# A hybrid attention and gating layer on one core: three kinds of 128-column matmul go from three rounded products to one unrounded product

## The chip, the cores and the metric

The kernel runs on 1 core of one Trainium2 chip. The time is device microseconds (us) of one execution; the median of 3 runs is 1607.43 us (1607.42 to 1607.93). The engines are named as in the profile: PE (TensorE matmuls), PEld (its weight loads), DVE (VectorE), ACT (ScalarE), POOL (GpSimd) and SP (SyncE, which here issues DMAs). A trailing q, as in SPq, is the engine's queue.

## The reference

One layer with 512 tokens of 2048 features and 16 heads, all in 32-bit floats. Cut to what matters:

```
proj = h @ w_in                       # q_lat, kv_lat, k_rope, z, u, v, ...
q    = rmsnorm(q_lat) @ w_uq          # 16 heads, 128 + 64 rotary
kv   = rmsnorm(kv_lat) @ w_ukv        # 16 heads, key 128 + value 128
s    = (q_nope . k_nope + q_rope . k_rope) / sqrt(192), causal, softmax -> p
A    = (p @ v) * silu(z_mla)
mixed = tril(W_s[g]) @ v_chunk + b_s  # 16 groups, 4 chunks of 128 tokens
B    = u * mixed * silu(z_sgu)
out  = rmsnorm(x + gate * ((sigmoid(g_mla) A + sigmoid(g_sgu) B) @ w_out))
```

The change touches three products: the gating mix (`tril(W_s) @ v_chunk`), the scores (`q_nope . k_nope`) and the product with the values (`p @ v`).

## The kernel before, in words

**Rounded pairs.** A 32-bit operand x is split into a rounded part h and the remainder l = x - h (`hilo`, L140: ACT copies x to h with rounding, then DVE subtracts). A product a·b is then three matmuls, ah·bh + ah·bl + al·bh, added up in PSUM (`mm3`, L135 to L138). Every operand that PE reads has to pass ACT and then DVE first. Two products, L441 and L1079, are done unrounded: one matmul instruction on 32-bit operands, which the trace shows as two records, each with its own weight load.

**The stages, in order of time.** To about 345 us: conditioning and the first projections. From 348 to about 1130 us: 266 *slots* (loop at L1276), in each of which PE does 16 or 24 matmuls (L1289 to L1297) of the rest of the input projection. From about 1137 to 1433 us: attention, one head after another (loop at L1523). Then the output projection.

**What orders the slots.** The side work on DVE and ACT is put into slots by a planner (`place`, L590). Each job brings a planned cost in us of DVE time, and goes to the first slot whose planned DVE time stays under 2.7 (2.6 for slots of 16 matmuls). Jobs are planned in this order: the gating mix of group pairs 7 and 0 (the others are pinned to one pair in about 35 slots), the rotary tables (`rope_make`, some 48 small DVE operations and three sines on ACT), the bias sums (`share`), the normalisation of the two latents (`lat_sq`, `lat_recip`, `lat_norm`, which go through DRAM and back), and the rotary key (`key_turn`, `key_rotary`: four transposes, five ACT copies and three DVE operations). Each job begins where the one before it ended, so a job that gets shorter pulls the later ones forward.

**One group pair of the gating mix** (L866 to L886): `v_load` brings the values of a group from DRAM, `sgu_weights` masks the two weight blocks, `sgu_weights_split` splits them, `sgu_scale` (ACT, four operations of 128 columns) applies the norm, `sgu_split` splits the values, `sgu_mix` does eight matmuls in two PSUM banks (L850 with both weight parts side by side, 256 columns; L851 with 128 columns), and `sgu_out` brings the result out in four DVE operations of 256 columns.

**One head of attention** (L1523 to L1558). PE's order: scores of the head; the query of the next head (and, before every second head, its rotary part); ten transposes of the probabilities; the key of the next head; the product with the values (`pv`); after every odd head the values of the next pair. Scores are causal in blocks of 128 queries: block i has (i+1)·128 key columns, so block 0 has 128 columns (L1423). In `pv` key block j has (4-j)·128 query columns, so block 3 has 128 (L1481). ACT and DVE split the query, the key, the transposed probabilities and the values between these steps. The trace gives all splits of this kind L141 (ACT) and L124 (DVE).

Of the kernel before, what the change touches and what calls it, by code (L numbers as in the profile page):

```python
# [116 lines left out]
def trunk_layer(ctx, tc, xT, xn, c, vecs, pos, wada, w1, w2, wv, wv3, wv4, wh, wh15, wq, wqr, wk, wvv, wo, wsT, bsp, gfin, out,  # L117
# [8 lines left out]
    def stt(out, in0, scalar, in1, op0, op1, **kw):  # L126
        DVE.scalar_tensor_tensor(out=out, in0=in0, scalar=scalar, in1=in1, op0=op0, op1=op1, **kw)  # L127
# [12 lines left out]
    def hilo(hi, lo, src):  # L140
        ACT.copy(hi, src)  # L141
        tt(lo, src, hi.bitcast(F32), ALU.subtract)
# [142 lines left out]
    def bank():  # L285
        n_bank[0] += 1
        return bank_at(ring[(n_bank[0] - 1) % len(ring)])
# [280 lines left out]
    def slot(name, dt=F32):  # L568
        return nt(latp.p, [P, S], dt, name)
# [248 lines left out]
        DMA.dma_start(br, bass.AP(tensor=bsp.tensor, offset=bsp.offset + p * 2 * P, ap=[[0, P], [P, 2], [1, P]]))  # L818

    def v_load(g):  # L820
        sgw["v"] = v = nt(latp.p, [P, NB, P], F32, "lat10")
        DMA.dma_start(v, v_d[:, :, g * P:(g + 1) * P].rearrange("n p w -> p n w"))

    def sgu_weights():
        wr = sgw["wr"]
        tt(wr, wr, tri.unsqueeze(1).broadcast_to([P, 2, P]), ALU.mult)

    def sgu_weights_split():
        wr = sgw["wr"]
        sgw["w"] = whl = nt(sg[0].p, [P, 2, 2 * P], F32R, "whl")  # L830
        hilo(whl[:, :, :P], whl[:, :, P:], wr)

    def sgu_scale():
        v = sgw["v"]
        for n in range(NB):
            ACT.activation(v[:, n], v[:, n], AF.Copy, scale=rv[:, n:n + 1])

    def sgu_split():
        v = sgw["v"]
        sgw["hl"] = [nt(latp.p, [P, NB, P], F32R, f"lat{i}") for i in (11, 12)]  # L840
        hilo(*sgw["hl"], v)

    def sgu_mix(q):
        whl, (vh, vl) = sgw["w"], sgw["hl"]
        sgw["ps", q] = []
        for half in range(2):
            ps = bank().rearrange("p (n w) -> p n w", n=2)
            for n2 in range(2):
                n = 2 * half + n2
                PE.matmul(ps[:, n2], vh[:, n, :], whl[:, q], start=True, stop=False)  # L850
                PE.matmul(ps[:, n2, :P], vl[:, n, :], whl[:, q, :P], start=False, stop=True)  # L851
            sgw["ps", q].append(ps)

    def sgu_out(g, half, part, tag):
        if half == part == 0:
            bs[g] = slot(tag)
        br = sgw["br"]
        gain = vec[:, C_GS + g:C_GS + g + 1]
        ps = sgw["ps", g % 2][half]
        o = bs[g][:, half * 256:(half + 1) * 256].rearrange("p (n w) -> p n w", n=2)  # L860
        if part == 0:
            stt(o, ps[:, :, :P], gain, br[:, g % 2].unsqueeze(1).broadcast_to([P, 2, P]), ALU.mult, ALU.add)
        else:
            stt(o, ps[:, :, P:], gain, o, ALU.mult, ALU.add)

    sgu_end, s_, e_ = {}, 2, -2  # L866
    for p in (7, 0, 1, 2, 3, 4, 5, 6):
        s_ = max(s_, 2 if p in (0, 7) else base[1 + 5 * p + 1])
        on(s_ - 3, LOAD, sgu_load, p)
        on(max(e_ + 1, s_ - 3), LOAD, bias_load, p)  # L870
        on(s_ - 3, LOAD, v_load, 2 * p)
        s_ = place(place(s_, 0.42, sgu_weights), 0.42, sgu_weights_split)
        for q in range(2):
            g = 2 * p + q
            on(s_ + 1, BACK, sgu_scale)
            s_ = place(s_ + 2, 0.69, sgu_split)
# [5 lines left out]
            for half in range(2):  # L882
# [446 lines left out]
    c1[0].close()  # L1329
    ga = Scope("G")  # L1330
    g2p = Scope("G2")
    gt, vt = [None] * H, [None] * H

    def fetch(h):
# [12 lines left out]
    def qproj(h, meanwhile=None):  # L1347
        wH, wL = get(gq[h])
        if meanwhile:
            meanwhile()  # L1350
        ps = bank()
        for k in range(6):
            sl = slice(k * P, (k + 1) * P)
            mm3(ps, wH[:, sl], wL[:, sl], lh[k], ll[k], k == 0, k == 5)
        qh, ql = at("qh", F32R), at("ql", F32R)
        hilo(qh, ql, ps)
        qt[h] = (qh, ql)

    def rproj(p):
        wH, wL = get(gr[p])  # L1360
# [24 lines left out]

    def kfinish(h, ps):
        kh, kl = at("kh", F32R), at("kl", F32R)
        hilo(kh, kl, ps)
        kt[h] = (kh, kl)

    def vproj(p):
        wH, wL = get(gvv[p])
        pss = []
        for t2 in range(2):
            ps = bank().rearrange("p (n w) -> p n w", n=2)
            for n in range(2):
                tk = slice((2 * t2 + n) * P, (2 * t2 + n + 1) * P)
                for k in range(4):
                    sl = slice(k * 256, (k + 1) * 256)
                    mm3(ps[:, n], lh[6 + k][:, tk], ll[6 + k][:, tk], wH[:, sl], wL[:, sl], k == 0, k == 3)  # L1400
            pss.append(ps)

        def finish():
            vv[p] = []
            for t2, ps in enumerate(pss):
                vh = at(f"vh{t2}", F32R, (P, 2, 256))
                vl = at(f"vl{t2}", F32R, (P, 2, 256))
                hilo(vh, vl, ps)
                vv[p].append((vh, vl))

        merging.insert(0, finish)

    def scores(h):
        qh, ql = qt.pop(h)
        kh, kl = kt.pop(h)
        q2 = qs.pop(h)
        s3, s2, s1 = bank(), bank(), bank()
        dst = {3: s3, 2: s2[:, :384], 1: s1[:, :256], 0: s1[:, 256:384]}
        for i in (3, 2, 1, 0):
            ps = dst[i]  # L1420
            n = (i + 1) * P
            q = slice(i * P, (i + 1) * P)
            mm3(ps, qh[:, q], ql[:, q], kh[:, :n], kl[:, :n], True, False)  # L1423

            PE.matmul(ps, q2[:, q], krh[:, :n], start=False, stop=False)  # L1425
            PE.matmul(ps, q2[:, q], krl[:, :n], start=False, stop=True)  # L1426
        return dst
# [28 lines left out]
    def transposes(pr_, js):  # L1456
        w = sum((NB - j) * P for j in js)
        ps = bank()[:, :w]
        o = 0
        for j in js:  # L1460
            for i in range(j, NB):
                PE.transpose(ps[:, o:o + P], pr_[i][:, j * P:(j + 1) * P], ident)  # L1462
                o += P
        th = at(f"th{js[0]}", F32R)[:, :w]
        tl = at(f"tl{js[0]}", F32R)[:, :w]
        parts = {}
        o = 0
# [4 lines left out]
        return parts, lambda: hilo(th, tl, ps)  # L1472

    mh, ml = [None] * H, [None] * H

    def pv(h, parts):
        ps = bank()
        hc = slice((h % 2) * P, (h % 2 + 1) * P)
        for j in range(NB):
            vh, vl = vv[h // 2][j // 2]  # L1480
# [42 lines left out]
    for h in range(H):  # L1523
        if h == H - 1:
            ring[:], n_bank[0] = [4, 5, 6, 7], 0
        dst = scores(h)
        more, odd = h + 1 < H, h % 2 == 1
        pair = h // 2 + 1
        first = go[0, 0] if not more else gr[pair] if not odd and 2 * pair < H else None
        pr_ = softmax(dst, (lambda: ws.split_to(first)) if first is not None else None)  # L1530
        if more:
            qproj(h + 1, lambda: merge(1 if h == H - 2 else None))
            if not odd and 2 * pair < H:
                rps = rproj(pair)
# [4 lines left out]
        pa, fa = transposes(pr_, (0,))  # L1539
        fa()  # L1540
        pb, fb = transposes(pr_, (1,))
        fb()
        pc, fc = transposes(pr_, (2, 3))
        fc()
# [6 lines left out]
        ops = pv(h, {**pa, **pb, **pc})  # L1551
# [7 lines left out]
    merge()  # L1559
    hp.close()  # L1560
    latp.close()

# [132 lines left out]
```

## Time and profile before

| | |
|---|---|
| median of 3 runs | 1607.43 us |
| the profiled execution's own time | 1607.38 us |
| its span, first to last instruction | 1605.7 us |
| mean granted PE clock | 0.998 |
| PE busy, share of the span | 99% |
| DVE, ACT busy | 75%, 47% |

How to read it. Matmuls are pipelined: a record of a matmul lasts from its start to a modelled end and overlaps with the next, so what a matmul costs is the distance from its start to the next start, not its duration. Where PE waits, the distance grows, and the record after the gap names what it waited for. Time that PE idles is all that side work can give back.

### The profile page before, as it was taken

The numbers are of one execution on the slowest core, as the hardware profiler recorded it, in microseconds if no ns is written. First come the engines' busy times: TensorE is split into PE (matmuls) and PEld (weight loads), VectorE is DVE, ScalarE is ACT, GpSimd is POOL, SyncE is SP. The second block draws the span as 40 slices with busy tenths as digits, with TensorE's granted clock in tenths as the row PEclk, the third lists the DMA queues.
The fourth block names the chain that finished last, engine by engine and source line by source line (L and its number), as shares of the span: only waits on it lengthen the run. The fifth ranks groups of instructions, "written<-read, shape, count | busy, mean of one in ns | idle before, by whom it ended". The sixth has DMA issues, their size and how long they took to land.

```text
span 1605.7 us, 25341 instructions
## 1 busy us (share of the span) xinstructions
PE 1586.8 (99%) x9848; PEld 1440.6 (90%) x9848; DVE 1210.6 (75%) x1833; ACT 755.4 (47%) x1259; POOL 105.1 (7%) x128
## 2 busy tenths in 40 slices
PE   9999999999999999999999999999999999999997
PEld 8888889999999999999999999999788889888887
DVE  8989679758787887778777787777778888764453
ACT  4443333454645454454545644645555555542322
POOL 0000000001111111111111111012000000000000
PEclk9999999999999999999999999999999999999999
DMA  9878489568799898898978879889322232336422
GB/s 380 354 293 321 171 280 323 173 188 208 206 246 263 220 252 229 210 261 220 232 198 249 242 199 253 255 210 236 129 90 85 84 104 89 93 110 225 135 88 105
DMA packets 122760, 329.54 MB, mean 205 GB/s; under 512 B 14072, under 2 KB 35600, under 8 KB 115856
## 3 DMA queue, kind: packets, MB, share of 16 engines
q1 hardware_dynamic: 104768, 269.72, 47.8%
q0 software_dynamic: 17872, 58.20, 20.7%
q8 instruction: 77, 1.26, 0.3%
q14 instruction: 43, 0.35, 0.1%
HBM read 303.95 MB, written 23.93 MB: 204 GB/s over the span
## 4 chain that ended last, share of the span: by engine, by line
PE 86%; DVE 6%; DMA 3%; ACT 3%; issue 2%; SPq 0%; DVEq 0%; ACTq 0%
PE ps L137 14%; PE ps L136 14%; PE ps L138 14%; PE ps L1289 11%; PE ps L1297 8%; PE ps L1295 8%; PE ps L1296 8%; PE ps L1291 6%; PE ps L1462 1%; DMA lat<-v_d 1%; DVE lat L124 1%; DVE wada L127 1%; PE ps L1425 1%; PE ps L1426 1%; DVE t L124 1%
## 5 line engine op out<-in xcount | busy, mean ns | idle before, releaser
L124 DVE TENSOR_TENSOR lat<-ps,lat 128x256 f32<-128x256 f32 (+1 forms) x238 | 112.1, 475 | 54.8 <-ACT lat L788 43.9
L107 DVE TENSOR_TENSOR w0l<-wraw,w0h 128x1024 fp32r<-128x1024 f32 (+3 forms) x74 | 78.9, 1066 | 58.1 <-ACT w0h L106 57.8
L106 ACT CAST w1h<-wraw 128x1024 fp32r<-128x1024 f32 (+3 forms) x74 | 63.8, 863 | 118.9 <-PE ps L138 57.5
L107 DVE TENSOR_TENSOR w1l<-wraw,w1h 128x1024 fp32r<-128x1024 f32 (+3 forms) x74 | 73.1, 988 | 61.6 <-ACT w1h L106 60.6
L106 ACT CAST w0h<-wraw 128x1024 fp32r<-128x1024 f32 (+3 forms) x74 | 68.9, 931 | 106.5 <-PE ps L138 66.7
L127 DVE SCALAR_TENSOR_TENSOR wada<-wada,cact 128x2048 f32<-128x2048 f32 x47 | 107.1, 2281 | 0.0
L136 PE MATMUL ps<-w0h,h 128*128 128x256 f32 (+3 forms) x288 | 92.7, 322 | 0.0
L137 PE MATMUL ps<-w0l,h 128*128 128x256 f32 (+3 forms) x288 | 92.6, 321 | 0.0
L138 PE MATMUL ps<-w0h,h 128*128 128x256 f32 (+3 forms) x288 | 92.4, 321 | 0.0
L136 PE MATMUL ps<-h,w1h 128*128 128x512 f32 x226 | 89.9, 398 | 1.1 <-ACT w1h L106 1.0
L137 PE MATMUL ps<-h,w1h 128*128 128x512 f32 x226 | 88.3, 391 | 0.8 <-DVE h L127 0.8
L138 PE MATMUL ps<-h,w1l 128*128 128x512 f32 x226 | 88.3, 391 | 0.0
L634 POOL DMA_DIRECT2D wraw<-in_wh x67 | 59.3, 940 | 435.6 <-DVE w0l L124 161.0
L124 DVE TENSOR_TENSOR w2l<-raw,w2h 128x1024 fp32r<-128x1024 f32 x56 | 68.5, 1223 | 17.7 <-ACT w2h L654 17.0
L136 PE MATMUL ps<-h,w0h 128*128 128x512 f32 x198 | 78.1, 395 | 2.0 <-DVE lat L124 2.0
L137 PE MATMUL ps<-h,w0h 128*128 128x512 f32 x198 | 77.2, 390 | 0.0
L138 PE MATMUL ps<-h,w0l 128*128 128x512 f32 x198 | 77.1, 390 | 0.0
L634 POOL DMA_DIRECT2D raw<-in_wh x42 | 39.6, 980 | 551.5 <-DVE raw L124 337.0
L124 DVE TENSOR_TENSOR w1l<-raw,w1h 128x1024 fp32r<-128x1024 f32 x45 | 55.1, 1224 | 26.5 <-ACT w1h L654 26.1
L124 DVE TENSOR_TENSOR lat<-lat,lat 128x512 f32<-128x512 f32 (+1 forms) x108 | 74.0, 685 | 0.7
L654 ACT CAST w2h<-raw 128x1024 fp32r<-128x1024 f32 x56 | 58.9, 1051 | 24.9 <-PE ps L1296 13.1
L124 DVE TENSOR_TENSOR w0l<-wraw,w0h 128x1024 fp32r<-128x1024 f32 x43 | 52.6, 1224 | 23.1 <-ACT w0h L654 22.7
(349 smaller groups left out, 5204.3 us busy)
## 6 DMA issues: line engine op xcount, KB each, us to landing
raw<-in_wh SPq DMA_DIRECT2D x105, 512.0 KB, 6.6
wada<-in_wada SPq DMA_DIRECT2D x47, 1024.0 KB, 7.1
wraw<-in_wh POOLq DMA_DIRECT2D x67, 512.0 KB, 7.4
wraw<-in_wh SPq DMA_DIRECT2D x45, 512.0 KB, 7.9
raw<-in_wh POOLq DMA_DIRECT2D x42, 512.0 KB, 8.7
wraw<-in_wo SPq DMA_DIRECT2D x32, 512.0 KB, 3.6
half<-in_w SPq DMA_DIRECT2D x35, 256.0 KB, 5.8
wraw<-in_w SPq DMA_DIRECT2D x16, 512.0 KB, 8.3
```

What stands on the lines that cost most here:

```text
L106: self.nc.scalar.copy(hi[:, :n], raw[:, :n])
L107: self.nc.vector.tensor_tensor(out=lo[:, :n], in0=raw[:, :n], in1=hi[:, :n].bitcast(F32), op=ALU.subtract)
L124: DVE.tensor_tensor(out=out, in0=in0, in1=in1, op=op)
L127: DVE.scalar_tensor_tensor(out=out, in0=in0, scalar=scalar, in1=in1, op0=op0, op1=op1, **kw)
L136: PE.matmul(ps, ah, bh, start=start, stop=False)
L137: PE.matmul(ps, ah, bl, start=False, stop=False)
L138: PE.matmul(ps, al, bh, start=False, stop=stop)
L634: q_.dma_start(t, wh[h, n, q // 10 - 1], **eng)
L1289: PE.matmul(both, wH[:, cols[c]], xs[c], start=c == 0 and first, stop=False, skip_group_check=True)
L1295: PE.matmul(ps[:, :256], wH[:, cols[c]], xh, start=c == 0 and first, stop=False, skip_group_check=True)
L1296: PE.matmul(ps[:, :256], wH[:, cols[c]], xl, start=False, stop=False, skip_group_check=True)
L1297: PE.matmul(ps[:, :256], wL[:, cols[c]], xh, start=False, stop=c == 7, skip_group_check=True)
```

## The change

- **Gating mix.** The masked weights and the scaled values are no longer split: `sgu_weights_split` and `sgu_split` go. `sgu_mix` is four unrounded matmuls of 128 columns in one PSUM bank, and `sgu_out` one DVE operation of 512 columns, planned at 0.75 instead of four at 0.48. Both groups of a pair load their values at the start of the pair, in two buffers (lat10, lat11).
- **Scores, block 0.** The first 128 columns of query and key are also copied unrounded (`q0`, `k0`, on ACT, ahead of the split), and block 0 is one unrounded matmul. The query's split shrinks to 384 columns; the key's stays at 512, since the other blocks use all of it.
- **Product with the values, block 3.** The last 128 columns of the transposed probabilities (`p3`) and the values of the last 128 tokens (`v3`) are copied unrounded on ACT, ahead of the split, and left out of it; block 3 is one unrounded matmul.

```diff
     def v_load(g):
-        sgw["v"] = v = nt(latp.p, [P, NB, P], F32, "lat10")
+        sgw["v", g % 2] = v = nt(latp.p, [P, NB, P], F32, f"lat{10 + g % 2}")
...
     def sgu_mix(q):
-                PE.matmul(ps[:, n2], vh[:, n, :], whl[:, q], start=True, stop=False)
-                PE.matmul(ps[:, n2, :P], vl[:, n, :], whl[:, q, :P], start=False, stop=True)
+        wr, v = sgw["wr"], sgw["v", q]
+        sgw["ps", q] = ps = bank().rearrange("p (n w) -> p n w", n=NB)
+        for n in range(NB):
+            PE.matmul(ps[:, n], v[:, n], wr[:, q], start=True, stop=True)
+
+    def sgu_out(g, tag):
+        bs[g] = slot(tag)
+        stt(bs[g].rearrange("p (n w) -> p n w", n=NB), sgw["ps", g % 2], vec[:, C_GS + g:C_GS + g + 1],
+            sgw["br"][:, g % 2].unsqueeze(1).broadcast_to([P, NB, P]), ALU.mult, ALU.add)
...
-        on(s_ - 3, LOAD, v_load, 2 * p)
-        s_ = place(place(s_, 0.42, sgu_weights), 0.42, sgu_weights_split)
+        for q in range(2):
+            on(s_ - 3, LOAD, v_load, 2 * p + q)
+        s_ = place(s_, 0.42, sgu_weights)
         for q in range(2):
             g = 2 * p + q
-            on(s_ + 1, BACK, sgu_scale)
-            s_ = place(s_ + 2, 0.69, sgu_split)
-            if q == 0:
-                on(s_, LOAD, v_load, g + 1)
+            on(s_ + 1, BACK, sgu_scale, q)
             s_ += 2
             on(s_, MISC, sgu_mix, q)
-            e_ = max(s_, e_) + 1
-            for half in range(2):
-                for part in range(2):
-                    e_ = place(e_, 0.48, sgu_out, g, half, part, ("cosT", "sinT")[q] if p == 7 else f"lat{8 + q}")
+            e_ = place(max(s_, e_) + 1, 0.75, sgu_out, g, ("cosT", "sinT")[q] if p == 7 else f"lat{8 + q}")
...
         qh, ql = at("qh", F32R), at("ql", F32R)
-        hilo(qh, ql, ps)
+        q0 = nt(full.p, [P, P], F32, "q0")
+        ACT.copy(q0, ps[:, :P])
+        hilo(qh[:, P:], ql[:, P:], ps[:, P:])
...
+        k0 = nt(full.p, [P, P], F32, "k0")
+        ACT.copy(k0, ps[:, :P])
         hilo(kh, kl, ps)
...
+            v3 = nt(full.p, [P, 256], F32, "v3")
+            ACT.copy(v3, pss[1][:, 1])
             for t2, ps in enumerate(pss):
-                hilo(vh, vl, ps)
+                n = 2 - t2
+                hilo(vh[:, :n], vl[:, :n], ps[:, :n])
...
-            mm3(ps, qh[:, q], ql[:, q], kh[:, :n], kl[:, :n], True, False)
+            if i > 0:
+                mm3(ps, qh[:, q], ql[:, q], kh[:, :n], kl[:, :n], True, False)
+            else:
+                PE.matmul(ps, q0, k0, start=True, stop=False)
...
+            n = w - P * (NB - 1 in js)
+            if n < w:
+                parts[NB - 1] = nt(full.p, [P, P], F32, "p3")
+                ACT.copy(parts[NB - 1], ps[:, n:])
+            hilo(th[:, :n], tl[:, :n], ps[:, :n])
...
-            mm3(ps[:, j * P:], vh[:, j % 2, hc], vl[:, j % 2, hc], parts[j][0], parts[j][1], j == 0, j == NB - 1)
+            else:
+                PE.matmul(ps[:, j * P:], vv[h // 2][2][:, hc], parts[j], start=False, stop=True)
```

**On PE, at the end of the scores of the first head.** Before (`lat` the query's and the key's rounded parts, `h` the rotary ones, the last two rows the next query):

```order
L1425 MATMUL ps_1499_12026<-h_1480_11863,h_1494_11963 128x256
L1426 MATMUL ps_1499_12026<-h_1480_11863,h_1494_11963 128x256
L136 MATMUL ps_1499_12026<-lat_1491_11955,lat_1488_11932 128x128
L137 MATMUL ps_1499_12026<-lat_1492_11956,lat_1488_11932 128x128
L138 MATMUL ps_1499_12026<-lat_1491_11955,lat_1489_11933 128x128
L1425 MATMUL ps_1499_12026<-h_1480_11863,h_1494_11963 128x128
L1426 MATMUL ps_1499_12026<-h_1480_11863,h_1494_11963 128x128
L136 MATMUL ps_1509_12088<-h_1467_11755,w1h_11968 128x512
```

After, at the same place (`k` and `q` are k0 and q0; L1410 and L1411 are the old L1425 and L1426):

```order
L1410 MATMUL ps_1445_11817<-h_1424_11647,h_1440_11754 128x256
L1411 MATMUL ps_1445_11817<-h_1424_11647,h_1440_11754 128x256
L1408 MATMUL ps_1445_11817<-k_1438_11746,q_1434_11721 128x128
L1410 MATMUL ps_1445_11817<-h_1424_11647,h_1440_11754 128x128
L1411 MATMUL ps_1445_11817<-h_1424_11647,h_1440_11754 128x128
L136 MATMUL ps_1456_11879<-h_1411_11540,w1h_11759 128x512
```

Three rounded matmuls of 128 columns have become one instruction on unrounded operands; nothing else moved on PE here.

**On ACT, over one head of attention** (an even one). Before: `b` the merged output of the head before, `lat` the query, `w1h` a weight split, `h`, `h` and `lat` the three banks of transposed probabilities, `w0h` a weight split, `lat` the key, then the turned rotary part:

```order
L141 CAST b_1562_12472<-sig_12342 128x512
L141 CAST lat_1565_12495<-ps_1564_12476 128x512
L106 CAST w1h_12499<-wraw_86_12310 128x512
L141 CAST h_1514_12141<-ps_1568_12524 128x512
L141 CAST h_1516_12148<-ps_1569_12531 128x384
L141 CAST lat_1571_12541<-ps_1570_12537 128x384
L106 CAST w0h_12545<-wraw_87_12355 128x768
L141 CAST lat_1574_12564<-ps_1573_12551 128x512
L1176 COPY h_1486_11902<-ps_1567_12505 32x512 x4
```

After:

```order
L141 CAST b_1516_12269<-sig_12139 128x512
L1331 COPY q_1521_12294<-ps_1518_12273 128x128
L141 CAST lat_1519_12292<-ps_1518_12273 128x384
L106 CAST w1h_12298<-wraw_86_12107 128x512
L141 CAST h_1462_11934<-ps_1523_12323 128x512
L141 CAST h_1464_11941<-ps_1524_12330 128x384
L1462 COPY p_1528_12342<-ps_1525_12336 128x128
L141 CAST lat_1526_12340<-ps_1525_12336 128x256
L106 CAST w0h_12346<-wraw_87_12152 128x768
L1365 COPY k_1532_12367<-ps_1529_12352 128x128
L141 CAST lat_1530_12365<-ps_1529_12352 128x512
L1149 COPY h_1430_11689<-ps_1522_12304 32x512 x4
```

Three copies of 128 columns have come in, each ahead of the split of the same bank; two of the splits are 128 columns narrower, the key's is as wide as before.

**On DVE, at the end of the slots.** Before (`rx<-lat,lat` is the last operation of the rotary key; `h<-b,vec,h` are the splits of the latents for attention; the last row empties the bank that the first query matmul writes next):

```order
L127 SCALAR_TENSOR_TENSOR h_1472_11794<-b_1452_11671,vec_88,h_1472_11794 128x512
L124 TENSOR_TENSOR lat_1434_11547<-ps_1473_11797,lat_1434_11547 128x256 x2
L124 TENSOR_TENSOR rx_11585<-lat_1459_11686,lat_1460_11687 128x512
L127 SCALAR_TENSOR_TENSOR h_1475_11821<-b_1453_11673,vec_88,h_1475_11821 128x512
L127 SCALAR_TENSOR_TENSOR h_1476_11824<-b_1454_11675,vec_88,h_1476_11824 128x512
L107 TENSOR_TENSOR w0l_11844<-wraw_75_11744,w0h_11843 128x768
L124 TENSOR_TENSOR lat_1434_11547<-ps_1433_11522,lat_1434_11547 128x256
```

After:

```order
L127 SCALAR_TENSOR_TENSOR h_1416_11579<-b_1398_11464,vec_88,h_1416_11579 128x512
L124 TENSOR_TENSOR lat_1382_11347<-ps_1417_11582,lat_1382_11347 128x256 x2
L127 SCALAR_TENSOR_TENSOR h_1419_11605<-b_1399_11466,vec_88,h_1419_11605 128x512
L127 SCALAR_TENSOR_TENSOR h_1420_11608<-b_1400_11468,vec_88,h_1420_11608 128x512
L107 TENSOR_TENSOR w0l_11628<-wraw_75_11529,w0h_11627 128x768
L124 TENSOR_TENSOR lat_1382_11347<-ps_1381_11322,lat_1382_11347 128x256
```

The rotary key's operation is gone from here: with the mix planned shorter, the planner ends the latents' normalisation at slot 218 instead of 253, and the three operations of the rotary key stand in slots 236 to 238 instead of 261, 262 and 265. The bias sums begin at slot 19 instead of 29, and the sines at slot 12 instead of 16.

More of the change, by code (lines that the diff above doesn't have):

```diff
@@ L826, in sgu_weights, with sgu_scale @@
         tt(wr, wr, tri.unsqueeze(1).broadcast_to([P, 2, P]), ALU.mult)
[L828 to L834, printed above, removed]
+    def sgu_scale(q):
+        v = sgw["v", q]
         for n in range(NB):
             ACT.activation(v[:, n], v[:, n], AF.Copy, scale=rv[:, n:n + 1])
[L838 to L841, printed above, removed]
     def sgu_mix(q):
-        whl, (vh, vl) = sgw["w"], sgw["hl"]
-        sgw["ps", q] = []
-        for half in range(2):
[L847 to L864, printed above, removed]
+        wr, v = sgw["wr"], sgw["v", q]
[6 more added lines that the diff above has]
+            sgw["br"][:, g % 2].unsqueeze(1).broadcast_to([P, NB, P]), ALU.mult, ALU.add)
     sgu_end, s_, e_ = {}, 2, -2
@@ L1331, in trunk_layer @@
     g2p = Scope("G2")
+    full = Scope("full")
     gt, vt = [None] * H, [None] * H
@@ L1387, in kfinish @@
         kh, kl = at("kh", F32R), at("kl", F32R)
+        k0 = nt(full.p, [P, P], F32, "k0")
+        ACT.copy(k0, ps[:, :P])
         hilo(kh, kl, ps)
-        kt[h] = (kh, kl)
+        kt[h] = (kh, kl, k0)
     def vproj(p):
@@ L1407, in finish @@
                 vl = at(f"vl{t2}", F32R, (P, 2, 256))
-                hilo(vh, vl, ps)
+                n = 2 - t2
+                hilo(vh[:, :n], vl[:, :n], ps[:, :n])
                 vv[p].append((vh, vl))
+            vv[p].append(v3)
         merging.insert(0, finish)
     def scores(h):
-        qh, ql = qt.pop(h)
-        kh, kl = kt.pop(h)
+        qh, ql, q0 = qt.pop(h)
+        kh, kl, k0 = kt.pop(h)
         q2 = qs.pop(h)
@@ L1471, in transposes, with finish @@
             o += n
-        return parts, lambda: hilo(th, tl, ps)
+        def finish():
+            n = w - P * (NB - 1 in js)
[3 more added lines that the diff above has]
+            hilo(th[:, :n], tl[:, :n], ps[:, :n])
+            return parts
+        return finish
     mh, ml = [None] * H, [None] * H
@@ L1479, in pv @@
         for j in range(NB):
-            vh, vl = vv[h // 2][j // 2]
-            mm3(ps[:, j * P:], vh[:, j % 2, hc], vl[:, j % 2, hc], parts[j][0], parts[j][1], j == 0, j == NB - 1)
+            if j < NB - 1:
+                vh, vl = vv[h // 2][j // 2]
+                mm3(ps[:, j * P:], vh[:, j % 2, hc], vl[:, j % 2, hc], parts[j][0], parts[j][1], j == 0, False)
+            else:
+                PE.matmul(ps[:, j * P:], vv[h // 2][2][:, hc], parts[j], start=False, stop=True)
         return ps
@@ L1538, in trunk_layer @@
                 out_granule(0, i, pso)
[L1539 to L1544, printed above, removed]
+        parts_ = {}
+        for js in ((0,), (1,), (2, 3)):
+            parts_.update(transposes(pr_, js)())
         if more:
@@ L1550, in trunk_layer @@
             out_granule(0, 2, pso)
-        ops = pv(h, {**pa, **pb, **pc})
+        ops = pv(h, parts_)
         merge_a(h, ops)
@@ L1559, in trunk_layer @@
     merge()
+    full.close()
     hp.close()
```

3 lines of the change are left out of this document (1 added, 2 removed).

## The prediction

> **What bounds the kernel now.** First the head of the page, the span and the engines' shares.
>
> ```profile
> span 1605.7 us, 25341 instructions
> ...
> PE 1586.8 (99%) x9848; PEld 1440.6 (90%) x9848; DVE 1210.6 (75%) x1833; ACT 755.4 (47%) x1259; POOL 105.1 (7%) x128
> ```
>
> PE is the bound nearly everywhere, so the change can gain in two ways only: PE gets less to do, or PE waits less. Where it waits shows the view by windows, cut at the stages. Columns: window, its length, then busy us (and records) of PE, PEld, DVE, ACT and POOL, granted clock, DMA share, GB/s.
>
> ```profile
> 348.00:440.00 92.00, 89.02 (x647) 83.92 (x647) 72.47 (x126) 52.79 (x87) 11.34 (x13) 1.00 0.77 196
> 440.00:990.00 550.00, 550.00 (x3990) 522.08 (x3990) 439.31 (x593) 276.56 (x407) 69.44 (x81) 1.00 0.89 233
> 990.00:1075.00 85.00, 84.24 (x607) 79.38 (x606) 65.88 (x89) 47.12 (x69) 10.29 (x12) 1.00 0.86 235
> 1075.00:1145.00 70.00, 65.67 (x433) 59.30 (x432) 53.48 (x72) 39.43 (x59) 11.38 (x11) 1.00 0.79 209
> 1145.00:1425.00 280.00, 279.78 (x1637) 249.15 (x1636) 223.81 (x475) 148.25 (x324) 0.00 (x0) 1.00 0.28 91
> ```
>
> Length minus PE busy is PE's idle time: 2.98 us in the early slots, none in the middle, 0.76 in the late slots, 4.33 at the turn from slots to attention, 0.22 in attention. In the middle and in attention only fewer PE microseconds count; at the two ends of the slots DVE and ACT count too. The clock is 1.00 throughout and gives nothing.
>
> **What a block costs on PE.** The timeline of PE at the end of one head's scores:
>
> ```profile
> 1153.64 0.22 PE L136 MATMUL ps<-lat,lat 128*128 128x128 f32 x1
> 1153.70 0.28 PE L137 MATMUL ps<-lat,lat 128*128 128x128 f32 x1
> 1153.81 0.27 PE L138 MATMUL ps<-lat,lat 128*128 128x128 f32 x1
> 1153.92 0.27 PE L1425 MATMUL ps<-h,h 128*128 128x128 f32 x1
> 1154.03 0.27 PE L1426 MATMUL ps<-h,h 128*128 128x128 f32 x1
> 1154.14 0.45 PE L136 MATMUL ps<-h,w1h 128*128 128x512 f32 x1
> 1154.43 0.40 PE L137 MATMUL ps<-h,w1h 128*128 128x512 f32 x1
> 1154.66 0.39 PE L138 MATMUL ps<-h,w1l 128*128 128x512 f32 x1
> ```
>
> A rounded 512 costs 1154.66 - 1154.43 = 0.23. From the first 128 to 1154.43 lie five narrow ones and one wide: 0.79 - 0.23 = 0.56, so 0.112 each. A quarter of 0.23 would be 0.058; the spacing of 0.11 is that of the weight loads, so a narrow matmul pays for its load. A block of three costs 0.336.
>
> The unrounded form occurs on PE at L441 with 512 columns, and on PEld at L1079:
>
> ```profile
> 99.08 1.02 PE L441 MATMUL ps<-cosT,ones 128*128 128x512 f32 x2
> 99.54 0.79 PE L136 MATMUL ps<-h,w0h 128*128 128x512 f32 x1
> 100.17 0.39 PE L137 MATMUL ps<-h,w0h 128*128 128x512 f32 x1
> 911.99 0.19 PEld L851 LDWEIGHTS ps<-whl,lat 128*128 128x128 f32 x1
> 912.12 0.30 PEld L1079 LDWEIGHTS ps<-rx,ones 128*128 128x128 f32 x2
> ```
>
> Two records: two loads (0.30 against 0.19 for one, so the second starts 0.11 after the first) and 100.17 - 99.08 - 0.23 = 0.86 us for 512 columns, 0.43 per record. At 128 columns a record would stream for 0.107 us, about as long as a load: two cost 2 x 0.11 = 0.22. So an unrounded block costs 0.22 against 0.336 and saves 0.112 us.
>
> [...]
>
> **Term 1, scores and values.** 16 heads x 2 blocks = 32 blocks x 0.112 = **-3.6 us**, on the path, since attention has 0.22 us of idle time. Bounds: with a third load's time somewhere (0.336) the gain is 0; with both loads hidden and the streams alone (2 x 0.107) it is 32 x 0.122 = -3.9. I take the spacing of the loads, which the rows show.
>
> What could cover it up is the new copies on ACT ahead of the splits. The tightest place I found is the key of the next odd head:
>
> ```profile
> 1202.37 0.59 ACT L141 CAST lat<-ps 128x512 fp32r<-128x512 f32 x1 [1.32 <-PE ps L138]
> 1202.99 0.69 DVE L124 TENSOR_TENSOR lat<-ps,lat 128x512 fp32r<-128x512 f32 x1 [0.92 <-ACT lat L141]
> 1204.31 0.40 PE L137 MATMUL ps<-lat,lat 128*128 128x512 f32 x1
> L836 ACT ACTIVATE lat<-lat,rv 128x128 f32<-128x128 f32 x64 | 20.5, 393 | 10.0 <-DMA lat<-v_d 10.0
> ```
>
> The key's remainder is ready at 1202.99 + 0.69 = 1203.68; PE reads it at 1204.31: slack 0.63, and 0.52 once the values' block ahead of it is 0.11 shorter. The copy of 128 columns isn't in the trace; the nearest row, ACT's L836 of that width, has 20.5 / 64 = 0.32 us, and the 0.59 of the 512 columns is the upper end. At 0.32 it is hidden with 0.20 to spare; at 0.59 PE would wait 0.07 in some of the heads, 16 x 0.07 = 1.1 us at most. The other copies stand ahead of splits that shrink by as many columns. I take 0.
>
> **Term 2, the mix on PE.** One group in the timeline:
>
> ```profile
> 372.20 0.28 PE L850 MATMUL ps<-whl,lat 128*128 128x256 f32 x1
> 372.32 0.22 PE L851 MATMUL ps<-whl,lat 128*128 128x128 f32 x1
> ...
> 373.08 0.45 PE L1289 MATMUL ps<-s,w1h 128*128 128x512 f32 x1
> ```
>
> Eight matmuls take 373.08 - 372.20 = 0.88 us; four unrounded ones take 4 x 0.22 = 0.88. **0**, +-0.03 per group, +-0.5 in all. In the mix, then, PE gains nothing: there were eight loads and there are eight.
>
> **Term 3, early slots.** Per group DVE loses the split of the values and three and a half of its exits:
>
> ```profile
> L127 DVE SCALAR_TENSOR_TENSOR lat<-ps,vec,lat 128x256 f32<-128x256 f32 x28 | 13.4, 479 | 0.1
> L124 DVE TENSOR_TENSOR lat<-lat,lat 128x512 fp32r<-128x512 f32 x16 | 11.0, 685 | 0.0
> 376.80 0.47 PE L1289 MATMUL ps<-h,w0h 128*128 128x512 f32 x1 [0.71 <-DVE lat L124]
> ```
>
> Split 0.69 plus four exits of 0.48 less one exit of 512 columns at 0.69 (the split's row has that width) is 1.9 us per group, some 30 us over all. From 440 to 990 that is worth nothing, since PE never idles there. Early it may help: the stall of 0.71 before 376.80 is PE waiting for DVE to empty a bank. Against it, the planner pulls the rotary tables (sines at slot 12 instead of 16) and the bias sums (19 instead of 29) into the room, so DVE and ACT are as full, over fewer slots. Ends: 0 and the whole 2.98. I take half, **-1.5**.
>
> **Term 4, late slots.** The latents' normalisation runs through DRAM in the chain of waits:
>
> ```profile
> 997.26 6.21 DMA latn_d<-sinT
> 1003.49 6.90 DMA sinT<-lat_d
> 1010.45 7.13 DMA lat<-v_d
> ```
>
> SP issues these in order, so the load of a mix group's values waits behind the load that waits for the store: 1010.45 + 7.13, and the scaling on ACT after it. This is most of the 0.76 idle. With the normalisation ending at slot 218 instead of 253 the same chain falls into an earlier pair, and the values are now loaded for both groups at its start. Ends: -0.8, and +1.5 if both loads of a pair wait behind it. I take **0**.
>
> **Term 5, the turn into attention.** The rotary key's operations stand among the last slots:
>
> ```profile
> 1108.99 0.59 ACT L1160 COPY rx<-ps 128x512 f32<-128x512 f32 x1 [1.94 <-PE ps L1158]
> 1116.05 0.47 PE L1289 MATMUL ps<-h,w0h 128*128 128x512 f32 x1 [1.34 <-DVE lat L124]
> 1122.26 0.69 DVE L124 TENSOR_TENSOR lat<-lat,sinT 128x512 f32<-128x512 f32 x1
> 1136.21 0.42 DVE L124 TENSOR_TENSOR lat<-ps,lat 128x256 f32<-128x256 f32 x1
> 1136.68 0.50 PE L136 MATMUL ps<-h,w0h 128*128 128x512 f32 x1 [1.99 <-DVE lat L124]
> ```
>
> PE waits 1.34 at 1116.05 and 1.99 at 1136.68, both for DVE emptying a bank. DVE has no pause from before 1122.26 to 1136.21; one rotary operation of 0.69 lies in that stretch, and the one that the order shows near its end is of the same shape. The copy of 0.59 at 1108.99 pushes back ACT's weight split, and so DVE's, ahead of the first stall. In the changed kernel these operations stand some 25 slots earlier, where PE doesn't wait. Moved away: 0.59 + 2 x 0.69 = 1.97. What is late next is the rest of DVE's queue, the latents' splits, which stay; and the room is 4.33. Ends 0 and -3.0; I take a little less than the sum, **-1.6**.
>
> **Sum.** Against the profiled execution: 1607.38 - 3.6 + 0 - 1.5 + 0 - 1.6 = **1600.7 us**; its 1607.38 is 0.05 under the median, which is no difference. A change of 0.2%, 3.2 us, is about what a measurement of this kernel can tell from none, so "faster" starts below 1604.2.
>
> **Rivals.**
>
> [...]
>
> *Only the blocks count.* The schedule gives nothing, because jobs move into the room, and the stalls at the ends are set by what stays: 1607.4 - 3.6 = **1603.8**. For it: terms 3 and 5 are half guesses, and averages of DVE mean nothing to a PE that waits for one bank. Chance 0.20.
>
> *A new stall behind the moved chain.* The store and reload of the latents (6.21 + 6.90) stands ahead of two value loads of a pair in SP's queue, PE waits for the mix, or DVE gets its jobs in a lump: two or so stalls of the size of 0.71 to 1.34, +1.8 together, and no other schedule gain: 1607.4 - 3.6 + 1.8 = **1605.6**. Against: loads are issued three slots before use, and the middle has shown no idle time. Chance 0.10.
>
> *All stalls go.* 1607.4 - 3.6 - 2.98 - 0.76 - 4.33 = **1595.7**. Against: the sines and the first weights stay where they are. Chance 0.10.
>
> **Numbers.** The forecast has 0.55. Its own range, from terms 3 to 5, is 1597 to 1603.5. With the second rival whole and the edges of the last two, 8 in 10 lie in 1596.5 to 1604.8. Faster than 1604.2: 0.55 + 0.10 + 0.13 of the second rival's 0.20, which lies only 0.4 below the line, = 0.78. Slower, the first rival: 0.05. The rest, 0.17, within 0.2%.
>
> **What would show it.** Term 1: the profile after has in a head's scores one record of two, x2, where three were, and 0.22 from its start to the next; the stretch of two heads gets 4 x 0.112 = 0.45 us shorter. Wrong if the spacing is 0.34 or more, or if an idle time behind ACT's copy of the key appears in attention. Term 2: 0.88 between the first mix matmul and the next slot's. Terms 3 to 5: PE's idle time in the same stages is near 1.5, 0.8 and 2.7 instead of 2.98, 0.76 and 4.33, and the middle still has none; wrong if waits for DVE of a microsecond stand at the same two places of the turn, or new ones behind a load of the values. The whole is wrong outside the range: a time above 1605 would mean that a cost is missing from the sum; one below 1596, that unrounded blocks stream faster than 0.107.

## The result and the profile after

| | before | after |
|---|---|---|
| median | 1607.43 us | 1596.72 us (1596.35 to 1596.85, 4 runs) |
| ratio | | 0.9933, 95% interval 0.9915 to 0.995 |
| span of the profiled execution | 1605.7 us | 1595.1 us |

10.7 us less, clearly faster by the 0.2% of the prediction; the forecast was 6.7 us less. The head of the page after:

```profile
span 1595.1 us, 25267 instructions
...
PE 1579.4 (99%) x9816; PEld 1434.7 (90%) x9816; DVE 1178.5 (74%) x1761; ACT 750.1 (47%) x1291; POOL 104.6 (7%) x128
```

The kernel after in the same windows as the kernel before:

```profile
348.00:440.00 92.00, 91.19 (x667) 86.57 (x666) 73.95 (x120) 51.32 (x82) 11.19 (x13) 1.00 0.89 230
440.00:990.00 550.00, 549.84 (x3988) 521.39 (x3987) 425.37 (x549) 275.99 (x398) 69.53 (x82) 1.00 0.88 236
990.00:1075.00 85.00, 85.00 (x618) 80.62 (x617) 57.89 (x74) 44.20 (x66) 11.04 (x13) 1.00 0.85 217
1075.00:1145.00 70.00, 67.24 (x457) 61.59 (x456) 53.08 (x72) 38.04 (x58) 10.54 (x10) 1.00 0.64 170
1145.00:1425.00 280.00, 279.80 (x1605) 247.75 (x1605) 217.26 (x476) 152.53 (x379) 0.00 (x0) 1.00 0.30 93
```

PE's idle time: early slots 0.81 (2.98 before), late slots 0 (0.76), turn 2.76 (4.33), attention 0.20 (0.22). DVE's busy time in the middle fell from 439.31 to 425.37 us and PE gained nothing from that.

The end of the first head's scores on PE, where three rounded matmuls stood:

```profile
1147.01 0.39 PE L1408 MATMUL ps<-k,q 128*128 128x128 f32 x2
1147.15 0.31 PE L1410 MATMUL ps<-h,h 128*128 128x128 f32 x1
1147.29 0.27 PE L1411 MATMUL ps<-h,h 128*128 128x128 f32 x1
1147.40 0.44 PE L136 MATMUL ps<-h,w1h 128*128 128x512 f32 x1
```

The block is one instruction of two records. The matmul behind it starts 0.14 after it and not 0.22, as the prediction had it for a sign; over the whole row of narrow matmuls the price shows: from the block's start to the next query 0.39 us pass, where it was 1154.14 - 1153.64 = 0.50. What a head is worth is read from the first transpose of the first head and of the last, before and then after:

```profile
1162.39 0.27 PE L1462 MATMUL ps<-ident,h 128*128 128x128 f32 x1
...
1430.34 0.27 PE L1462 MATMUL ps<-ident,h 128*128 128x128 f32 x1
```

```profile
1155.65 0.27 PE L1447 MATMUL ps<-ident,h 128*128 128x128 f32 x1
...
1419.88 0.27 PE L1447 MATMUL ps<-ident,h 128*128 128x128 f32 x1
```

267.95 against 264.23 us for 15 heads: 0.248 per head, 0.124 per block.

The mix, one group:

```profile
372.91 1.06 PE L837 MATMUL ps<-wsr,lat 128*128 128x128 f32 x8
373.72 0.47 PE L1262 MATMUL ps<-s,w1h 128*128 128x512 f32 x1
```

Eight records as before, in 0.81 instead of 0.88 us; the first wide matmul behind them gives half of that back (0.32 us from its start to the next, where it was 0.28), and over a stretch that holds it too a group is 0.035 shorter, 16 x 0.035 = 0.56 us in all.

And the places where PE waits at the turn:

```profile
1110.77 0.47 PE L1262 MATMUL ps<-h,w0h 128*128 128x512 f32 x1 [0.86 <-DVE lat L124]
...
1130.07 0.50 PE L136 MATMUL ps<-h,w0h 128*128 128x512 f32 x1 [0.90 <-DVE lat L124]
...
1135.48 0.50 PE L136 MATMUL ps<-h,w1h 128*128 128x512 f32 x1 [1.00 <-ACT w1h L106]
```

The first two were 1.34 and 1.99 in these rows; the third waits for ACT's split of the key's weights and is as long as before (1.00 at 1142.10).

**Where the 10.5 us of the span went.** Counted from start to start, less the usual spacing: attention 16 x 0.248 = 4.0; the early stalls, six before (0.96 at 354, 0.87 at 376, 0.42 at 398, 0.52 at 407, 0.70 at 411, 0.47 at 433 us, together 3.93 before rounding) and one after (0.97 at 354), 3.0; the mix on PE 0.6; the late stall 0.92 at 1025 us, of which a new one of 0.32 near 919 us takes back a part, 0.6; the turn 0.5 + 1.1 = 1.6. That is 9.8; the start of the slots is 0.2 earlier, and the rest, 0.5, is by my estimate the tenth of a microsecond by which PE runs slower behind each of the stalls that went: in the kernel before the matmul behind the one at 376.80 us starts 0.31 after it and not 0.23, and behind the one at 1025.08 us 0.22 after it and not 0.12.

### The profile page after: what moved, and what is told of

Its sections match the earlier page's. It is cut to its first block, busy times and chain, and to the rows that moved or that the text cites. A ratio compares the mean times of both kernels' runs of the same rounds, so it can differ in the third digit from the quotient of the medians.

```text
span 1595.1 us, 25267 instructions
## 1 busy us (share of the span) xinstructions
PE 1579.4 (99%) x9816; PEld 1434.7 (90%) x9816; DVE 1178.5 (74%) x1761; ACT 750.1 (47%) x1291; POOL 104.6 (7%) x128
## 4 chain that ended last, share of the span: by engine, by line
PE 90%; DVE 4%; DMA 2%; ACT 2%; issue 1%; SPq 0%; DVEq 0%; ACTq 0%
PE ps L136 14%; PE ps L138 14%; PE ps L137 14%; PE ps L1262 12%; PE ps L1270 9%; PE ps L1269 8%; PE ps L1268 8%; PE ps L1264 6%; PE ps L1447 1%; PE ps L837 1%; DVE wada L127 1%; DVE t L124 1%; PE ps L1411 1%; DMA wraw<-in_w 1%; PE ps L1410 1%
## 5 line engine op out<-in xcount | busy, mean ns | idle before, releaser
L124 DVE TENSOR_TENSOR lat<-ps,lat 128x256 f32<-128x256 f32 (+2 forms) x238 | 107.7, 456 | 52.2 <-ACT lat L788 40.1
L124 DVE TENSOR_TENSOR w0l<-raw,w0h 128x1024 fp32r<-128x1024 f32 x46 | 56.3, 1224 | 17.0 <-ACT w0h L654 16.2
```

What stands on the lines that cost most here:

```text
L124: DVE.tensor_tensor(out=out, in0=in0, in1=in1, op=op)
```

## The experiments

Each edit is against the changed kernel unless it says otherwise. The kernel before was run beside them on each chip; its medians there were 1607.8 to 1608.0 us.

**1. The parts alone** (mix_alone: the diff up to `sgu_out` and its planning; att_alone: the rest).

> The gating mix of the changed kernel with the attention of the kernel before. If the parts only add up (ours): the attention's 3.7 us are missing, 1596.7 + 3.7 = 1600.4 us, and PE's idle time from 348 to 1145 us is as short as in the changed kernel. Rival, the attention's shorter blocks are what pulls the stalls away: nothing before 1137 us can then differ from the kernel before but PE's 0.6 us of the mix, 1606.8 us.

> The gating mix of the kernel before with the attention of the changed kernel. Ours: 32 blocks at 0.116 us less each and nothing else, 1607.4 - 3.7 = 1603.7 us, the slots' stalls all still there. Rival, the copies cost something that the mix's lighter load hides: more than 1604.5 us.

Measured: 1600.57 us (ratio 0.9955, 0.9939 to 0.9972) and 1604.18 us (0.9977, 0.9968 to 0.9987). Beside the runs of before on their chip that is 7.4 and 3.8 us less, 11.2 together against 10.7: the parts add up. Attention's share is the block price alone, as the fifteen heads of att_alone take 264.3 us, against 264.2 in the changed kernel; the slots' share is the mix alone.

**2. The old plan with the new mix** (old_plan), and the same with DVE's old load (old_load).

```diff
...
-        for q in range(2):
-            on(s_ - 3, LOAD, v_load, 2 * p + q)
-        s_ = place(s_, 0.42, sgu_weights)
+        on(s_ - 3, LOAD, v_load, 2 * p)
+        s_ = place(place(s_, 0.42, sgu_weights), 0.42, nothing)
...
+            s_ = place(s_ + 2, 0.69, nothing)
+            if q == 0:
+                on(s_, LOAD, v_load, g + 1)
             s_ += 2
             on(s_, MISC, sgu_mix, q)
-            e_ = place(max(s_, e_) + 1, 0.75, sgu_out, ...)
+            e_ = place(max(s_, e_) + 1, 0.48, sgu_out, ...)
+            for _ in range(3):
+                e_ = place(e_, 0.48, nothing)
...
```

`nothing` only reserves planned time; the second group's values are loaded later again, too, as in the kernel before. In old_load each `nothing` is a DVE operation on scratch data (512 columns for the split, 256 for an exit and for the weights), which the output does not use. DVE then has a little more to do than in the kernel before, since the real exit has 512 columns (0.75 us) where that kernel's first exit has 256 (0.48).

> The changed kernel, but the planner still reserves the time of the operations that are gone, so that the rotary tables, the bias sums, the latents and the rotary key stand in the slots of the kernel before. Ours (the early stalls go because DVE has less to do there, the turn's because the rotary key has left it): the early stalls stay away, the turn's come back, 1596.7 + 1.6 = 1598.3 us. Rival (the early stalls go because the jobs stand in other slots): all of them come back, and only PE's gains in attention and in the mix are left, 1607.4 - 3.7 - 0.6 = 1603.1 us.

> The kernel with the old plan, 1600.5 us, and on DVE operations on scratch data of the same widths in the places of those that the change took away, so that DVE has the load of the kernel before while PE has the unrounded mix. Ours (the early stalls come from DVE's load): they come back, 1600.5 + 2.6 = 1603.1 us. Rival (they come from what PE or ACT did for the rounded mix): 1600.5 us.

Measured: 1600.50 us (0.9954, 0.9939 to 0.9969) and 1602.17 us (0.9963, 0.9949 to 0.9976). Neither theory's number. In the early slots of old_plan one stall behind DVE is left, besides the one near 354 us that waits for ACT in all of them:

```profile
423.97 0.38 PE L1277 MATMUL ps<-s2h,w2l 128*128 128x256 f32 x1 [0.55 <-DVE w2l L124]
```

In old_load there are three, two of them at the bank emptying where the kernel before has 0.71 and its like:

```profile
376.44 0.47 PE L1278 MATMUL ps<-h,w0h 128*128 128x512 f32 x1 [0.30 <-DVE lat L124]
...
397.83 0.47 PE L1278 MATMUL ps<-h,w2h 128*128 128x512 f32 x1 [0.29 <-DVE lat L124]
...
432.07 0.39 PE L1286 MATMUL ps<-s1h,w0l 128*128 128x256 f32 x1 [0.48 <-DVE w0l L124]
```

By the start of the same slot near 449 us, when each of them has done the mix of four groups, the kernel after is 3.6 us ahead of before (counted from the start of the slots), old_plan 2.7, old_load 1.5. By these differences DVE's load is worth 1.2 of the 3.6, the other places of the jobs 0.8, and 1.5 come with things that old_load also has: no splits of values and weights on ACT, and 0.1 of PE's mix. Which of ACT's operations it is was not tried. The trace of the kernel before has a candidate: DVE waits twice for ACT around the split of the mix's weights, old_load's DVE has neither wait, and PE's stalls of 0.52 and 0.70 at 407 and 411 us behind them are missing there.

```profile
400.32 0.43 DVE L124 TENSOR_TENSOR whl<-wsr,whl 128x256 fp32r<-128x256 f32 x1 [0.47 <-ACT whl L141]
...
401.79 1.23 DVE L124 TENSOR_TENSOR w0l<-wraw,w0h 128x1024 fp32r<-128x1024 f32 x1 [0.58 <-ACT w0h L654]
```

Each of these shares is a difference of single executions. The ten profiled executions that have the new mix and the new plan agree within 0.1 us on this stretch. The two that have the old early slots don't: att_alone is 1.8 us later there than the kernel before, most of it behind a load of the mix's weights for which DVE waits 1.81 us at 401.23, where the kernel before waits 0.26. So the 3.6 hold against this execution of the kernel before, and the shares are less firm than their sum.

The turn and the late slots agree with the plan: old_plan has the late stall of 0.92 and the two of the turn, 1.50 and 2.14, back in full. The late one in the kernel before:

```profile
1025.08 0.39 PE L1297 MATMUL ps<-s1h,w1l 128*128 128x256 f32 x1 [0.76 <-DVE w1l L124]
```

**3. Only the rotary key back at the end** (key_late).

```diff
-    s_ = max(s_lat + 1, sgu_end[6])
+    s_ = max(s_lat + 1, sgu_end[6], 254)
```

> The changed kernel with only the rotary key put back to the end of the slots, where the kernel before has it. Ours: the stalls of the turn grow from 1.0 and 1.1 to about 1.5 and 2.1, 1596.7 + 1.5 = 1598.2 us. Rival, the turn's stalls shrank because DVE and ACT reach the turn with less backlog: no change, 1596.7 us.

Measured: 1598.99 us (0.9946, 0.9931 to 0.9961). The stalls are 1.50 and 2.16 again, so the rotary key's place is what shrank them. The second is followed by something that the kernel before does not show:

```profile
1130.19 0.39 PE L138 MATMUL ps<-h,w1l 128*128 128x512 f32 x1
1132.58 0.53 PE L136 MATMUL ps<-h,w0h 128*128 128x512 f32 x1 [2.00 <-DVE lat L124]
1132.91 0.63 PE L137 MATMUL ps<-h,w0h 128*128 128x512 f32 x1
1133.34 0.63 PE L138 MATMUL ps<-h,w0l 128*128 128x512 f32 x1
```

The matmuls behind it are 0.43 apart instead of 0.23, eight of them; the windows view of the same kernel has the clock:

```profile
1129.00:1132.58 3.58, 1.58 (x8) 0.96 (x7) 3.58 (x7) 0.02 (x1) 0.00 (x0) 1.00 0.17 69
1132.58:1136.33 3.75, 3.75 (x10) 2.93 (x11) 3.17 (x5) 3.70 (x7) 0.00 (x0) 0.54 0.57 188
1136.33:1140.00 3.67, 3.67 (x18) 2.97 (x17) 1.25 (x2) 2.97 (x6) 0.00 (x0) 1.00 0.96 333
```

The granted clock is 0.54 on average over these 3.75 us. This costs 8 x 0.2 = 1.6 us, and covers the third wait of 1.16, which does not appear here: 0.4 us net.

**4. A block of 256 columns unrounded** (block1: q0, k0 256 wide, `if i > 1`).

> The changed kernel with block 1 of the scores (256 columns) unrounded too, copies of 256 columns. Ours (a record of an unrounded matmul takes the longer of its load, 0.11, and its stream, 0.43 for 512 columns): 2 x 0.215 = 0.43 against 3 x 0.12 = 0.36, 16 x 0.07 = +1.1, 1597.8 us. Rival (two records instead of three always save a third): 16 x 0.12 = -1.9, 1594.8 us.

Measured: 1598.25 us (0.994, 0.9925 to 0.9955), a head 0.095 us longer, 1.5 in all. On PE:

```profile
1146.36 0.59 PE L1408 MATMUL ps<-k,q 128*128 128x256 f32 x2
1146.61 0.47 PE L1410 MATMUL ps<-h,h 128*128 128x256 f32 x1
1146.91 0.28 PE L1411 MATMUL ps<-h,h 128*128 128x256 f32 x1
1147.03 0.39 PE L1408 MATMUL ps<-k,q 128*128 128x128 f32 x2
```

From block 1 to block 0 0.67 us pass, 0.60 in the kernel after (1146.41 to 1147.01). The second record of the block starts 0.22 after the first, where it is 0.11 at 128 columns with a weight load of the same size (the two records together take 0.59 us, and 0.39 at 128 columns): at 256 columns streams, not loads, set the price here, and the gain has turned into a loss. Of the two widths only 128 columns pay.

**5. The copies** (five_copies: k0's copy five times; copies_behind: the copies of q0 and k0 behind `hilo` instead of ahead of it).

> The changed kernel with the copy of the key made five times: 4 x 0.16 = 0.64 us more on ACT ahead of the key's split. Ours: the split has 0.35 us to spare before the odd heads and far more before the even ones, so 8 x 0.3 = +2.4, 1599.1 us, and the waits stand at the scores of the odd heads. Rival, one copy was already on the path: 16 x 0.64 = +10, 1607 us. Rival, there is much more room: 1596.7 us.

> The changed kernel with the copies of query and key made behind the splits instead of ahead of them. Ours: the copies are hidden where they stand, no difference beyond 0.3 us, 1596.7 us. Rival, the copy ahead of the split costs its 0.16 us before each odd head at least: 8 to 16 x 0.16, 1594.1 to 1595.4 us.

Measured: 1604.96 us (0.9982, 0.9973 to 0.9992) and 1602.71 us (0.9967, 0.9956 to 0.9979). Both expectations of mine fell, the first in size, the second altogether. ACT in five_copies:

```profile
1160.28 1.46 ACT L1366 COPY k<-ps 128x128 f32<-128x128 f32 x5 [1.27 <-PE ps L138]
1161.63 0.59 ACT L141 CAST lat<-ps 128x512 fp32r<-128x512 f32 x1
```

Five copies into one tile hold the split back by 1.35, where one holds it back by 0.17, so the dose was 1.18 and not 0.64. PE then waits 1.0 us longer ahead of the scores of each odd head, and nowhere else: with one copy some 0.2 us are left to spare there.

ACT in copies_behind, at the query of an even head:

```profile
1169.68 0.47 ACT L141 CAST lat<-ps 128x384 fp32r<-128x384 f32 x1
1171.00 0.27 ACT L1332 COPY q<-ps 128x128 f32<-128x128 f32 x1 [0.85 <-DVE lat L124]
```

The copy only reads the bank, but stands still until DVE's remainder has read it, 0.85 us, and ACT's queue with it: the split of the transposed probabilities, and then of the weights of the values. PE pays at the values of every second head:

```profile
1174.83 0.39 PE L137 MATMUL ps<-w0l,h 128*128 128x256 f32 x1 [0.34 <-DVE w0l L107]
```

0.74 us per pair of heads, 5.2 us in the span. That the copies stand ahead of the splits is worth more than attention's whole gain. What makes the copy stand still is in the trace: it carries a wait for the semaphore that DVE's operations raise, where the same copy in the changed kernel waits for PE's alone. So it is the program's semaphores that put one reader of the bank behind the other; that the bank by itself would hold a reader up is not shown.

**6. The stalls that are left at the turn.** turn: splits of latents 6 and 7 and the copies of the first rotary part later. last_turn: one slot moved. key_split: the rotary key's split next to its last operation. both: the last two. The edits of last_turn and key_split:

```diff
-            turn_ = [(1, k), (6, k), (2, k), (3, k - 1), (4, k - 1), (3, k), ...
+            turn_ = [(1, k), (6, k), (3, k - 1), (2, k), (4, k - 1), (3, k), ...
...
+    def key_split():
+        kr.extend([slot("lat12", F32R), slot("lat11", F32R)])
+        hilo(kr[4], kr[5], kr[0])
+
+    place(s_ + 1, 0.69, key_split)
...
-    krh, krl = at("krh", F32R), at("krl", F32R)
-    hilo(krh, krl, kr[0])
+    krh, krl = kr[4], kr[5]
```

> The changed kernel with two moves at the turn: the splits of latents 6 and 7, which only the key needs, go behind the end of the slots, and the four ACT copies of the first rotary part go behind the first query's matmuls. If DVE's and ACT's order is what holds PE there: the stalls of 1.06 and 1.16 us go, 1596.7 - 2.2 = 1594.5 us. Rival, the operations are only late elsewhere (the key's projection waits for the latents' splits, or the rotary part for its copies): 1596.7 us.

> The changed kernel with one slot moved in the last round of the order, so that the slots which accumulate in one bank, 3 and 4 of the last pair but one, no longer follow each other directly. If the stall of 1.02 us at 1110 is PE waiting for that bank: it goes, 1595.7 us. Rival, DVE is late there by its queue, and PE waits the same elsewhere: 1596.7 us.

> The changed kernel with the split of the rotary key (ACT 0.60, DVE 0.68) taken from behind the slots to the slot behind its last operation. If the wait of 1.16 us for the key's weights is ACT's queue: it shrinks by 0.6, 1596.1 us. Rival, the turn is bounded by DVE's queue ahead of that: 1596.7 us.

> Both moves, the slot and the rotary key's split. If they add up: 1596.7 - 1.0 - 0.6 = 1595.1 us. Rival, the slot that no longer stalls brings PE earlier to the turn and it waits there instead: 1596.1 us or more.

| | median, us | ratio, interval |
|---|---|---|
| turn | 1597.72 | 0.9936, 0.9921 to 0.9951 |
| last_turn | 1595.03 | 0.9919, 0.9905 to 0.9932 |
| key_split | 1596.87 | 0.9931, 0.9918 to 0.9945 |
| both | 1594.30 | 0.9914, 0.9901 to 0.9928 |

turn comes out as its rival had it: the waits at 1130 and 1135 us only moved, to the key's weights (0.30) and the values'.

```profile
1138.17 0.39 PE L136 MATMUL ps<-w0h,h 128*128 128x256 f32 x1 [0.82 <-ACT w0h L106]
1139.43 0.38 PE L137 MATMUL ps<-w0l,h 128*128 128x256 f32 x1 [0.87 <-DVE w0l L107]
```

Moving a slot helps, since it takes a wait away and nothing comes in its place: the 1.02 at 1110 is gone, and the next one shrinks from 1.06 to 0.28, as PE gets to the turn no earlier than DVE. This is 0.7 us more than I expected of it. In the kernel called both the wait for the key's weights is half as long, too:

```profile
1129.01 0.50 PE L136 MATMUL ps<-h,w0h 128*128 128x512 f32 x1
...
1133.91 0.50 PE L136 MATMUL ps<-h,w1h 128*128 128x512 f32 x1 [0.50 <-ACT w1h L106]
```

Between the late slots and the first transposes last_turn gains 1.9 us on the changed kernel, key_split 0.5 and both 2.4: they add up. By its median key_split alone is not told from the changed kernel; its 0.5 stand in the rows of one execution only. The median of both is 13.7 us below the kernel before on its chip, 3.0 more than the change alone, and it is the lowest of all; between both and last_turn the intervals overlap.

## Why the prediction was right or wrong

The direction was right, and so was the mechanism in the terms that the experiments could single out. The forecast was 4 us too high: 1596.72 lies just below the forecast's own range of 1597 to 1603.5, and only 0.2 above the low end of 1596.5 to 1604.8. The step that missed is the size of the early stalls, term 3.

- **Term 1, the blocks:** -3.6 forecast, -4.0 measured, a little beyond the bound of -3.9 for streams alone. Two records and two loads, as the rows of the two forms gave; 0.124 per block instead of 0.112. "Slower", chance 0.05, is out: the trace of the changed kernel has no third load in a block (two take 0.31 us on PEld at 1146.89, where one takes 0.19), and block1 shows the stream's price at 256 columns.
- **The copies at nothing:** right for one copy, but in part by luck: I had 0.2 us to spare for a copy of 0.32; 0.2 is what is left, but the copy holds the split back by only 0.17, so there was less cover than I worked out. What I didn't see is that the cover holds only where the copy stands: behind the split the copies cost 5.2 us.
- **Term 2, the mix on PE:** 0 forecast with +-0.5, -0.56 measured, a little outside that.
- **Term 3, early slots:** this is the term that was mis-sized. -1.5 forecast, at most -2.98; 3.0 of stalls went, and PE was 3.6 ahead at the end of the stretch. Two errors: I took half of the idle time because the jobs that move in would fill DVE again, and they do (73.95 us of the 92 are busy, 72.47 before), but PE no longer waits for it. And the upper end was PE's idle time in the windows view, 2.98, where the stalls counted from start to start are 3.93, because a matmul's modelled end reaches into the gap (at 376.80 us 0.87 from start to start less the usual spacing, 0.71 idle in the row). old_plan and old_load divide the gain: 1.2 for DVE's load, 0.8 for the jobs' places, and 1.5 whose cause stays open; what ACT no longer does is likely, not shown. DVE's load, on which the term rests, is thus only a part of what took the stalls away, the more so as old_load's exit of 512 columns is heavier than the one it stands for (0.75, which I had at 0.69, against 0.48).
- **Term 4, late slots:** 0 forecast, -0.6: the late stall of 0.92 went with the chain through DRAM, and a smaller one came. In old_plan both the chain and the stall are back, though other jobs moved back with them. The chain holds more than I priced: behind the three transfers ACT takes 1.28 us twice for a table load, at 1018.90 and 1020.90, around the root of the norm. The changed kernel has the same two at 932.47 and 934.82, where PE waits for neither.
- **Term 5, the turn:** -1.6 forecast, -1.6 measured, and key_late shows the rotary key to be the cause. My own sign against it, waits of a microsecond for DVE at the same two places, is there all the same: 1.02 and 1.06 from start to start, 0.86 and 0.90 idle, which fits the 2.7 us of idle time that I left at the turn. The first of them needs two slots that accumulate in one bank next to each other, as last_turn shows; the prediction had no reason for what stayed. The third wait, which I didn't count on, stayed as well.

"Only the blocks count", chance 0.20, the second rival of the forecast's numbers, fell with the early slots; "all stalls go", chance 0.10, 1595.7 us, came nearer to the time than the forecast did, but by coincidence, since 3.2 us of stalls at the turn and the early one of 0.97 are still there: the stalls were longer than the idle time by which I priced them, and the blocks and the mix gave more.

## What to carry to other kernels

Where PE is bound by loads of narrow blocks, price a form by its records: here each took the longer of its load (0.11) and its stream (0.22 at 256 columns), so 128 columns gained (2 x 0.11 against 3 x 0.112) and 256 lost (2 x 0.22 against 3 x 0.12). A stall's worth is the distance from start to start, not the idle time between modelled ends (3.93 against 2.98 us in the early slots here), and how busy an engine is over a stretch does not say whether the engine behind it waits (DVE 72.47 us before and 73.95 after, PE idle 2.98 and 0.81). Where the program's semaphores put the readers of a PSUM bank one behind the other, a second reader belongs ahead of the first pair, not behind it (5.2 us here).

## What the runs showed of the hardware

PE's granted clock halved behind a stall of 2 us in three of five profiled executions that have one at the turn. In key_late, old_plan and att_alone the stall of about 2.15 us (1.98 to 2.00 idle in the row) is followed by a granted clock of 0.50 for 3.41 us; in key_late matmuls of 512 columns start 0.43 us apart there instead of 0.23. The kernel before has the same stall in its profiled execution (1.99) and none of it, and nor has old_load (1.98):

```profile
1133.00:1136.68 3.68, 1.70 (x8) 1.08 (x6) 3.65 (x8) 0.02 (x1) 0.00 (x0) 1.00 0.11 43
1136.68:1140.00 3.32, 3.32 (x14) 2.74 (x15) 3.18 (x5) 3.28 (x6) 0.00 (x0) 1.00 0.54 173
```

The stall's length does not decide this, but where it falls fits all five. The half clock begins 0.03 us behind the end of the stall in att_alone, 0.32 in key_late and 1.16 in old_plan. The one stretch of full clock that the trace records lasts 1594.02 us in the kernel before and 1587.20 in the kernel after, 467 and 465 times 3.4133, so I counted in steps of 3.4133 us from the clock's changes. Laid over the stall, the 3.41 us that end where the clock halves hold the whole of it in these three. In old_plan:

```profile
1131.16:1134.56 3.40, 1.42 (x7) 0.98 (x6) 3.30 (x6) 1.18 (x3) 0.00 (x0) 1.00 0.00 0
1134.57:1137.97 3.40, 3.40 (x10) 2.63 (x9) 2.11 (x4) 3.34 (x7) 0.00 (x0) 0.50 0.84 273
```

In the kernel before the full clock ends at 1600.76 us, and 136 of these steps ahead of that, at 1136.55 us, a limit would cut the stall in two, with 1.85 us of idle time on the fuller side; in old_load the same count gives 1.38. The limits inside these two stalls are my estimate, since the clock does not change there. In these five executions, then, the same stall cost the 1.6 us more or not by where it fell. No threshold comes out of these traces: at the very end of key_split the clock halves behind 1.72 us of idle. The changed kernel, with 0.90 idle at the turn, shows none of it (1.00 from 1130.00 to 1133.40 us).
